# A decoder layer whose matmul order is fixed by hand: ScalarE and VectorE join the fixed order

## The chip, the cores and the metric

The kernel runs on one core of a Trainium2 chip. The metric is the time on the device in microseconds (us) of one execution. Engine names: TensorE (PE in the profile, PEld its weight loads), VectorE (DVE), ScalarE (ACT), GpSimd (POOL), SyncE (SP).

## The reference

One hybrid decoder layer in float32: 256 tokens, width 2048, and a memory of 256 rows.

```python
def reference(x, mem, ...):
    h = x
    h = h + 0.5 * swiglu(rmsnorm(h, g_ffn1), w1_gate, w1_up, w1_down)     # 2048 -> 2 x 5632 -> 2048
    z = rmsnorm(h, g_mix) @ w_in                                          # columns u, v, q, k, v
    y_a = spatial_gating(z[..., :2048], g_v, w_s, b_s)                    # gelu(u) * (causal w_s @ rmsnorm(gelu(v)) + b_s)
    y_b = window_attention_sinks(z[..., 2048:3072], k, v, sinks)          # 16 heads of 64, window 128
    y = concatenate([rmsnorm(y_a, g_a_out), rmsnorm(y_b, g_b_out)])
    h = h + y @ w_out
    h = h + cross_attention(rmsnorm(h, g_x), rmsnorm(mem, g_mem), w_xq, w_xkv, w_xo)   # 4 heads of 512
    h = h + 0.5 * swiglu(rmsnorm(h, g_ffn2), w2_gate, w2_up, w2_down)
    return rmsnorm(h, g_final)
```

## The kernel before

**Precision and tiles.** Each float32 operand is split into a high part (`...h`, a ScalarE cast to fp32r, line 148) and a low part (`...l`, VectorE's difference, line 149); a product takes three passes: high times high, low times high, high times low. The 256 tokens are two blocks of 128. Weights come in chunks of 1 MB (tile 128 x 2048, four pieces of 512 columns), loaded on SP's queue by `load`, which also splits them.

**Units.** A unit is one pass over the chunks of a weight for 1024 output columns by 256 tokens, in four or more PSUM banks named P, Q, R. Three kinds of chunk: N and C have 24 matmuls of 128x512, S has 21 (a seven-product scheme; its `t` tiles are sums of weight pieces). A unit's eight chunks go through `push` and `flush`: `push` of chunk i loads and splits it, then writes the matmuls of chunk i - 1; the last chunk's matmuls come with the `flush()` at the end of `unit`. Only after that do the lines behind `unit(...)` evict the banks (ScalarE with a scale or Gelu, or VectorE's additions), and the next unit's first `push` follows. In the first and last chunk of a unit the matmuls go bank by bank, so the third matmul needs the low part of the weights; in the others the passes with the low part come last.

**Sequence.** f1g (gate and up, 11 units), f1d (down), q, kv, v, u, mv0, mv1, mk0, mk1 (memory values and keys), wo, xq (2 units), xo, f2g, f2d. Between them lie `side` generators (transposes, attention, norms) of which `side_step` runs a piece at every sixth matmul; `yield n` puts the next piece n steps later. In units v, u and mv0 these are the window attention (scores `sc`, softmax in `scs`, transposes `pT`, copies `pTs`, products `wop`) and, in u, the normalised memory pairs `mT` by `pair_normalized`.

**What sets the order.** `tc.manual_schedule(engines={PE})`: TensorE's instructions run in program order. The order on ScalarE, VectorE, GpSimd and the DMA queues is a scheduler's, by dependencies and priorities (`tc.high_priority()` stands around the evictions); it may place an instruction ahead of others written before it. Within each engine's built order the hardware's queue is worked off from the front.

**The first unit.** `plain_gu_unit` works on `n0`, x in transposed form without the norm factor, while `prep1(i)` loads `xT` pairs and x itself into `h`, squares it (`parts1`), makes the norm factor and scales rows (`n1s`) for the units that follow.

Of the kernel before, what the change touches and what calls it, by code (L numbers as in the profile page):

```python
# [14 lines left out]
P = 128  # L15
T = 256
# [5 lines left out]
NEG = -1e30  # L22
NG = D // 512


# [5 lines left out]
def layer_kernel(  # L31
# [22 lines left out]
    nc = tc.nc  # L54
    ctx.enter_context(tc.manual_schedule(engines={mybir.EngineType.PE}))

# [18 lines left out]
    def s2(s):  # L75
        return tmp.tile([P, 512], F32, tag="s2", name=nm(s))
# [163 lines left out]

    def pair_from_dram(s, srcT, i, gcol, base=None, raw=None):
        if raw is None:
            raw = s2(s + "r").rearrange("p (k t) -> p k t", k=2)
            nc.sync.dma_start(raw, srcT[i * T:(i + 1) * T, :].rearrange("(k p) t -> p k t", p=P))
# [7 lines left out]
    def pair_normalized(s, kind, srcT, i, gcol, by_token):  # L252

        raw = s2(s + "r").rearrange("p (k t) -> p k t", k=4)
        src = srcT[i * T:(i + 1) * T, :].rearrange("(k p) t -> p k t", p=P)
        for tb in range(TB):
            a, b = laid(kind, 0, tb), laid(kind, 1, tb)
            nc.gpsimd.dma_start(raw[:, a:b + 1:b - a, :], src[:, :, tb * P:(tb + 1) * P])
        turned = 1 if kind == "S" else 0
        for k in range(2):  # L260
            c = gcol + 2 * i + k
            o = row_tile(kind, raw, k)
            nc.vector.scalar_tensor_tensor(
                out=o, in0=o, scalar=sm[:, c:c + 1], in1=by_token[:, turned:turned + 2, :],
                op0=ALU.mult, op1=ALU.mult,
            )
        p = Pair(s, kind)
        fill(s, p, raw)
        return p
# [28 lines left out]
    def load(s, w, kind, pieces):  # L298
# [5 lines left out]
        if kind == "S":  # L304
# [256 lines left out]
    def ffn(s, get, rs, wgu, wd, on_block, first=None):  # L561
# [36 lines left out]
        def gu_unit(c):  # L598
# [12 lines left out]
            for i in range(8):  # L611
                if c == 10 and i > 1:
                    inner(i - 2)
                push(
                    u, i, wgu[i, c], lambda i=i: get(i),
                    lambda i=i: seven_early(u, got) if i == 6 else late(u) if i == 7 else None,
                )
# [46 lines left out]
    def next_norm(s, gcol, kinds="NNNNNNNN"):  # L664
# [11 lines left out]
        def on_block(j, tb):  # L676
            square_into(parts[:, tb, j:j + 1], h[:, tb, j * 512:(j + 1) * 512], 512)
            done[j] += 1
            if not mixed:
                if done[j] == TB:  # L680
                    make(j, lambda tb, c: h[:, tb, c:c + P])
            elif j < 2:
                if done[0] + done[1] == 2 * TB:
                    st["est"] = rstd_of(parts[:, :, :2], 2, 1024)
                    for i in range(2):
                        scaled(i)
            elif done[j] == TB:
                scaled(j)
# [44 lines left out]

    quad = []

    def prep1(i):
# [4 lines left out]
        n0.append(pair_from_dram(  # L741
            "n0", xT, i, G_FFN1, [t[:, i % 2] for t in quad], raw=raw0 if i == 0 else None
        ))
        if i in (2, 3):
            for j in (2 * i - 4, 2 * i - 3):
                hj = h[:, :, j * 512:(j + 1) * 512]
                nc.sync.dma_start(hj, x[:, j * 512:(j + 1) * 512].rearrange("(b p) d -> p b d", p=P))
                for tb in range(TB):
                    square_into(parts1[:, tb, j:j + 1], hj[:, tb, :], 512)
        if i == 4:  # L750
            rs1.append(rstd_of(parts1, NG, D))
        if i >= 4:
            j = i - 4
            r = m4("n1s").rearrange("p (b c) -> p b c", b=TB)
            for tb in range(TB):
                nc.scalar.activation(
                    r[:, tb], h[:, tb, j * 512:(j + 1) * 512], AF.Copy, scale=rs1[0][:, tb:tb + 1]
                )

            def work():  # L760
                for q in range(2):
                    yield 3 if q == 0 else 1
                    n1[2 * j + q] = pair_from_rows(
                        "n1", KINDS[2 * j + q],
                        lambda tb, k: r[:, tb, (2 * q + k) * P:(2 * q + k + 1) * P],
                        G_FFN1 + 4 * j + 2 * q,
                    )

            side_add(work())

# [4 lines left out]
    )  # L775
    mT = []
    partsm = tiny.tile([P, TB, NG], F32, tag="parts", name=nm("parts"))

    def mem_squares(j):
        for tb in range(TB):  # L780
            mr = s2("mr")
            nc.gpsimd.dma_start(mr, mem[tb * P:(tb + 1) * P, j * 512:(j + 1) * 512])
            square_into(partsm[:, tb, j:j + 1], mr, 512)
# [27 lines left out]

    side_add(queries())
    rsm = rstd_of(partsm, NG, D)
    by_token = const.tile([P, 3, P], F32, name="by_token")

    def spread():

        dg = s2("dg")[:, :T].rearrange("p (b t) -> p b t", b=TB)
        for tb in range(TB):
# [138 lines left out]
    rsv = rstd_of(partsv, 2, DA)  # L958
    for tb in range(TB):
        nc.vector.scalar_tensor_tensor(  # L960
            out=v[tb], in0=v[tb], scalar=rsv[:, tb:tb + 1], in1=gv, op0=ALU.mult, op1=ALU.mult
        )
# [13 lines left out]
    def y_pairs(s, rows_, parts, gcol, k0):  # L976
        rs = rstd_of(parts, 2, DA)
        for tb in range(TB):
            nc.vector.tensor_scalar_mul(rows_[tb], rows_[tb], rs[:, tb:tb + 1])
# [171 lines left out]
    for cb in range(2):  # L1151
        both = rows_scaled("xq", unit("xq", w_xq, cb, n3), rs3_())
        for j in range(2):
            side_add(attend_memory(2 * cb + j, both[j]))

    n4, on4, rs4_ = next_norm("n4", G_FFN2, KINDS)
    for cb in range(2):
# [115 lines left out]
```

## Time and profile before

| what | before |
|---|---|
| time, median of 3 runs | 2107.73 us (2104.63 to 2107.79) |
| profiled execution, its own time | 2105.79 us |
| its span | 2104.0 us |
| its mean granted TensorE clock | 0.996 |

The span is what the profiler saw from the first to the last instruction; 1.8 us lie around it. Rows of the timeline give start and duration in us, then engine, line, operation, output from inputs, shape, and, in brackets, how long the engine was idle before and what ended that. Rows that group instructions give minimum, median and maximum in ns. TensorE's durations overlap, since matmuls are pipelined; the distance of their starts is what counts.

### The profile page before, as it was taken

The numbers are of one execution on the slowest core, as the hardware profiler recorded it, in microseconds if no ns is written. First come the engines' busy times: TensorE is split into PE (matmuls) and PEld (weight loads), VectorE is DVE, ScalarE is ACT, GpSimd is POOL, SyncE is SP. The second block draws the span as 40 slices with busy tenths as digits, with TensorE's granted clock in tenths as the row PEclk, the third lists the DMA queues.
The fourth block names the chain that finished last, engine by engine and source line by source line (L and its number), as shares of the span: only waits on it lengthen the run. The fifth ranks groups of instructions, "written<-read, shape, count | busy, mean of one in ns | idle before, by whom it ended". The sixth has DMA issues, their size and how long they took to land.

```text
span 2104.0 us, 23815 instructions
## 1 busy us (share of the span) xinstructions
PE 2076.0 (99%) x9527; PEld 1715.5 (82%) x9527; DVE 1674.5 (80%) x1609; ACT 1135.4 (54%) x1109; POOL 32.2 (2%) x51
## 2 busy tenths in 40 slices
PE   9999999999999999999999999999999999999998
PEld 7888888888888888788888888778888888888886
DVE  5888888888987745867858657798888888889878
ACT  7655555555544645544545455665555545555444
POOL 0000000000000000100000000000000000000000
PEclk9999999999999999999999999999999999999999
DMA  7555555555555554435555543455555555555553
GB/s 281 195 189 213 200 195 184 209 188 199 202 199 206 201 210 166 167 140 200 180 180 184 197 160 140 163 197 200 181 207 197 204 191 200 200 200 200 200 198 122
DMA packets 60110, 402.15 MB, mean 191 GB/s; under 512 B 6864, under 2 KB 8928, under 8 KB 12768
## 3 DMA queue, kind: packets, MB, share of 16 engines
q1 hardware_dynamic: 57280, 393.50, 51.7%
q0 software_dynamic: 2016, 6.30, 0.9%
q8 instruction: 74, 1.21, 0.2%
q10 hardware_dynamic: 704, 0.84, 0.1%
q14 instruction: 36, 0.29, 0.0%
HBM read 398.52 MB, written 2.10 MB: 190 GB/s over the span
## 4 chain that ended last, share of the span: by engine, by line
PE 94%; DVE 3%; ACT 1%; issue 1%; DMA 1%; POOL 0%; SPq 0%; POOLq 0%; DVEq 0%; ACTq 0%
PE f2gQ L363 16%; PE f1gQ L363 15%; PE f1dQ L363 6%; PE f2dQ L363 6%; PE f2gP L363 6%; PE f1gP L363 5%; PE f1dP L363 3%; PE f2dP L363 3%; PE woQ L363 2%; PE xqQ L363 2%; PE f1dR L363 2%; PE f2dR L363 2%; PE xoQ L363 2%; PE mk0Q L363 1%; PE mv1Q L363 1%; PE mv0Q L363 1%
## 5 line engine op out<-in xcount | busy, mean ns | idle before, releaser
L149 DVE TENSOR_TENSOR f1gwl<-f1gw,f1gwh 128x2048 fp32r<-128x2048 f32 (+1 forms) x91 | 185.5, 2043 | 51.6 <-ACT f1gwh L148 51.4
L148 ACT CAST f2gwh<-f2gw 128x1536 fp32r<-128x1536 f32 (+1 forms) x88 | 154.4, 1755 | 133.4 <-PE f2gQ L363 96.6
L148 ACT CAST f1gwh<-f1gw 128x2048 fp32r<-128x2048 f32 (+1 forms) x91 | 156.1, 1716 | 123.5 <-PE f1gQ L363 90.4
L149 DVE TENSOR_TENSOR f2gwl<-f2gw,f2gwh 128x1536 fp32r<-128x1536 f32 (+1 forms) x88 | 183.7, 2088 | 40.3 <-ACT f2gwh L148 40.2
L363 PE MATMUL f2gQ<-f2gwh,n4fh 128*128 128x512 f32 x363 | 141.4, 390 | 0.0
L363 PE MATMUL f2gQ<-f2gwh,n4fl 128*128 128x512 f32 x363 | 141.3, 389 | 0.0
L363 PE MATMUL f1gQ<-f1gwh,n1fh 128*128 128x512 f32 x330 | 128.6, 390 | 0.0
L363 PE MATMUL f1gQ<-f1gwh,n1fl 128*128 128x512 f32 x330 | 128.4, 389 | 0.0
L148 ACT CAST f2dwh<-f2dw 128x2048 fp32r<-128x2048 f32 (+1 forms) x44 | 79.2, 1799 | 91.2 <-PE f2dQ L363 71.2
L148 ACT CAST f1dwh<-f1dw 128x2048 fp32r<-128x2048 f32 (+1 forms) x44 | 79.2, 1799 | 87.9 <-PE f1dQ L363 68.2
L149 DVE TENSOR_TENSOR f2dwl<-f2dw,f2dwh 128x2048 fp32r<-128x2048 f32 (+1 forms) x44 | 94.4, 2145 | 27.0 <-ACT f2dwh L148 24.3
L363 PE MATMUL f2gQ<-f2gwl,n4fh 128*128 128x512 f32 x363 | 115.7, 392 | 0.0
L149 DVE TENSOR_TENSOR f1dwl<-f1dw,f1dwh 128x2048 fp32r<-128x2048 f32 (+1 forms) x44 | 94.3, 2144 | 26.8 <-ACT f1dwh L148 24.2
L363 PE MATMUL f1gQ<-f1gwl,n1fh 128*128 128x512 f32 x330 | 105.1, 392 | 0.0
L149 DVE TENSOR_TENSOR f2gtl<-f2gt,f2gth 128x2048 fp32r<-128x2048 f32 x33 | 75.6, 2292 | 17.0 <-ACT f2gth L148 16.6
L149 DVE TENSOR_TENSOR f1gtl<-f1gt,f1gth 128x2048 fp32r<-128x2048 f32 x30 | 68.8, 2292 | 18.3 <-ACT f1gth L148 18.0
L363 PEld LDWEIGHTS f2gQ<-f2gwh,n4fl 128*128 128x128 f32 x363 | 68.1, 188 | 14.2
L363 PEld LDWEIGHTS f2gQ<-f2gwh,n4fh 128*128 128x128 f32 x363 | 68.2, 188 | 14.1
L363 PEld LDWEIGHTS f2gQ<-f2gwl,n4fh 128*128 128x128 f32 x363 | 67.3, 188 | 13.5
L148 ACT CAST f2gth<-f2gt 128x2048 fp32r<-128x2048 f32 x33 | 63.1, 1913 | 23.1 <-DVE f2gt L314 18.3
L363 PEld LDWEIGHTS f1gQ<-f1gwh,n1fl 128*128 128x128 f32 x330 | 62.0, 188 | 12.9
L363 PEld LDWEIGHTS f1gQ<-f1gwh,n1fh 128*128 128x128 f32 x330 | 62.0, 188 | 12.8
(703 smaller groups left out, 5715.1 us busy)
## 6 DMA issues: line engine op xcount, KB each, us to landing
f2gw<-in_w_gu SPq DMA_DIRECT2D x88, 1024.0 KB, 4.8
f1gw<-in_w_gu SPq DMA_DIRECT2D x87, 1024.0 KB, 4.8
f1dw<-in_w_down SPq DMA_DIRECT2D x44, 1024.0 KB, 4.8
f2dw<-in_w_down SPq DMA_DIRECT2D x44, 1024.0 KB, 4.8
wow<-in_w_out SPq DMA_DIRECT2D x16, 1024.0 KB, 4.8
xqw<-in_w_xq SPq DMA_DIRECT2D x16, 1024.0 KB, 4.8
xow<-in_w_xo SPq DMA_DIRECT2D x16, 1024.0 KB, 4.8
qw<-in_w_in SPq DMA_DIRECT2D x8, 1024.0 KB, 5.0
```

The source lines that it names most:

```text
L148: nc.scalar.copy(hi, src)
L149: nc.vector.tensor_tensor(lo, src, hi.bitcast(F32), ALU.subtract)
L363: nc.tensor.matmul(self.banks[name], x, y, start=name not in self.begun, stop=self.left[name] == 0)
```

## The change

ScalarE and VectorE are added to the engines that follow program order. Since the program's order then decides when they do something, some of the program is moved:

- `prep1`: x goes into `h` in four DMAs from GpSimd at i = 1 to 4 (before: two by two from SyncE at i = 2, 3); the next `xT` pair is loaded one step ahead; the norm factor is made at i = 5, the scaling of rows (`normalized`) at i = 6 and 7, two blocks each.
- `load`, kind S: the three additions for `t` stand ahead of the split of the other pieces.
- `ffn`: the norm factor is taken at chunk 5 of the first unit; `next_norm` scales the first two blocks in a side generator, two steps later.
- q unit: `beside_queries` loads rows of `mem` a step ahead of their squares and takes the norm factor at i = 3; the last squares come behind the unit. `spread` and `y_pairs` begin with a `yield 2`.
- u unit: `beside_u` scales v at i = 1; the `memT` blocks are loaded a chunk ahead of the pair that uses them, so that the last two pairs fall into mv0.
- xq: the norm factor is taken at i = 3. `shared.clear()` is called twice more.

```diff
+PINNED = {mybir.EngineType.PE, mybir.EngineType.DVE, mybir.EngineType.Activation}
-    ctx.enter_context(tc.manual_schedule(engines={mybir.EngineType.PE}))
+    ctx.enter_context(tc.manual_schedule(engines=PINNED))
...
     def load(s, w, kind, pieces):
...
-            split(wh[:, 1:, :], wl[:, 1:, :], raw[:, 1:, :])
             nc.vector.tensor_tensor(
                 t[:, 0:2, :], raw[:, 1:3, :], raw[:, 0:1, :].to_broadcast([P, 2, 512]), ALU.add
             )
             nc.vector.tensor_tensor(t[:, 2, :], t[:, 0, :], raw[:, 2, :], ALU.add)
             nc.vector.tensor_tensor(t[:, 3, :], t[:, 2, :], raw[:, 3, :], ALU.add)
+            split(wh[:, 1:, :], wl[:, 1:, :], raw[:, 1:, :])
             split(th, tl, t)
...
     def prep1(i):
...
+        raw = ahead.pop()
+        if i < 7:
+            ahead.append(s2("n0r").rearrange("p (k t) -> p k t", k=2))
+            nc.sync.dma_start(ahead[0], rows_of(xT, i + 1))
+        n0.append(pair_loaded("n0", raw, i, G_FFN1, [t[:, i % 2] for t in quad]))
+        if 1 <= i <= 4:
+            cols = slice((i - 1) * 512, i * 512)
+            nc.gpsimd.dma_start(h[:, :, cols], x[:, cols].rearrange("(b p) d -> p b d", p=P))
+        if 2 <= i <= 5:
+            for tb in range(TB):
+                square_into(parts1[:, tb, i - 2:i - 1], h[:, tb, (i - 2) * 512:(i - 1) * 512], 512)
+        if i == 5:
+            rs1.append(rstd_of(parts1, NG, D))
+        for j in {6: (0, 1), 7: (2, 3)}.get(i, ()):
+            normalized(j)
...
-    pq = unit("q", w_in, 2, n2, lambda i: mem_squares(i // 2) if i % 2 else None)
+    pq = unit("q", w_in, 2, n2, beside_queries)
...
+    def beside_u(i):
+        if i == 1:
+            for tb in range(TB):
+                nc.vector.scalar_tensor_tensor(
+                    out=v[tb], in0=v[tb], scalar=rsv[:, tb:tb + 1], in1=gv, op0=ALU.mult, op1=ALU.mult
+                )
+        beside_mT(i)
+
+    def beside_mT(i):
+        if loaded:
+            mT[i - 2] = pair_normalized("mT", KINDS[i - 2], loaded.pop(), i - 2, G_MEM, by_token)
+        if 1 <= i <= 8:
+            loaded.append(load_blocks("mT", KINDS[i - 1], memT, i - 1))
...
-    pu = unit("u", w_in, 0, n2, lambda i: mT.append(pair_normalized("mT", KINDS[i], memT, i, G_MEM, by_token)))
+    pu = unit("u", w_in, 0, n2, beside_u)
...
-    pv_ = unit("mv0", w_xkv, 2, mT)
+    pv_ = unit("mv0", w_xkv, 2, mT, lambda i: beside_mT(8 + i) if i < 2 else None)
```

Where work lands on the engines is read from the built instruction orders. ScalarE where unit v ends and u begins, before (`v` the Gelu evictions, `junk` the squares, `uwh` u's weights; line numbers are those of each kernel's own file):

```order
L148 CAST vwh_6006<-vw_6005 128x2048
L148 CAST uwh_6124<-uw_6123 128x2048
L900 ACTIVATE scs_6026,den_5861<-scs_6026,nmx_6032 128x128 x4
L956 ACT_TABLE_LOAD
L956 ACTIVATE v_5731<-vP_997_5746,rs_5557 128x512
L956 ACTIVATE v_5731<-vQ_998_5747,rs_5557 128x512
L138 ACTIVATE junk_6088,partsv<-v_5731 128x512
L138 ACTIVATE junk_6091,partsv<-v_5731 128x512
L956 ACTIVATE v_5732<-vR_5748,rs_5557 128x512
L148 CAST uwh_6145<-uw_6144 128x2048
L138 ACTIVATE junk_6094,partsv<-v_5732 128x512
L956 ACTIVATE v_5732<-vQ_1000_5749,rs_5557 128x512
```

And in the changed kernel at the same place:

```order
L985 ACTIVATE v_5731<-vP_997_5746,rs_5359 128x512
L140 ACTIVATE junk_6088,partsv<-v_5731 128x512
L985 ACTIVATE v_5731<-vQ_998_5747,rs_5359 128x512
L140 ACTIVATE junk_6091,partsv<-v_5731 128x512
L985 ACTIVATE v_5732<-vR_5748,rs_5359 128x512
L140 ACTIVATE junk_6094,partsv<-v_5732 128x512
L985 ACTIVATE v_5732<-vQ_1000_5749,rs_5359 128x512
L140 ACTIVATE junk_6097,partsv<-v_5732 128x512
L150 CAST uwh_6109<-uw_6108 128x2048
L150 CAST uwh_6120<-uw_6119 128x2048
```

Both of u's first casts stood ahead of v's last eviction; now both stand behind it and behind the last square.

ScalarE where u ends and mv0 begins, before (`u` the evictions, `scs` exponentials of the window attention, `mT` pairs of the normalised memory):

```order
L900 ACTIVATE scs_6451,den_6257<-scs_6451,nmx_6457 128x256 x2
L148 CAST mTfh_6472<-mTr_6467 128x512
L148 CAST mv0wh_6638<-mv0w_6637 128x2048
L148 CAST mTfh_6474<-mTf_6476 128x512
L969 ACT_TABLE_LOAD
L969 ACTIVATE u_6107<-uP_1073_6150,rs_5557 128x512
L969 ACTIVATE u_6107<-uQ_1074_6151,rs_5557 128x512
```

And in the changed kernel:

```order
L929 ACTIVATE scs_6592,den_6230<-scs_6592,nmx_6598 128x256 x2
L1009 ACT_TABLE_LOAD
L1009 ACTIVATE u_6105<-uP_1064_6125,rs_5359 128x512
L1009 ACTIVATE u_6105<-uQ_1065_6126,rs_5359 128x512
L1009 ACTIVATE u_6106<-uR_6127,rs_5359 128x512
L1009 ACTIVATE u_6106<-uQ_1067_6128,rs_5359 128x512
L150 CAST mTfh_6612<-mTr_6504 128x512
L150 CAST mTfh_6614<-mTf_6616 128x512
L150 CAST mv0wh_6628<-mv0w_6627 128x2048
```

The first cast for mv0 stood ahead of u's evictions; now it stands behind all four, behind two casts of an `mT` pair, and these behind the exponentials of the last scores (`scs_6592`), whose scores TensorE computes after u's last matmul.

VectorE where mv1 ends and mk0 begins, before (`mv` the sums that evict mv1, `mk0wl` the low part of mk0's first weights):

```order
L149 TENSOR_TENSOR mk0wl_7298<-mk0w_7296,mk0wh_7297 128x2048
L484 TENSOR_TENSOR mv1v_7258<-mv1Q_1251_7105,mv1p_1270_7257 128x512
L490 TENSOR_TENSOR mv_6635<-mv1P_1236_7031,mv1p_1270_7257 128x512
L485 TENSOR_TENSOR mv1z_7259<-mv1Q_1250_7104,mv1v_7258 128x512
L310 TENSOR_TENSOR mk0t_7340<-mk0w_7336 128x1024
```

And in the changed kernel:

```order
L497 TENSOR_TENSOR mv1v_7260<-mv1Q_1239_7034,mv1v_7260 128x512
L498 TENSOR_TENSOR mv_6609<-mv1Q_1240_7035,mv1v_7260 128x512
L499 TENSOR_TENSOR mv_6608<-mv1Q_1241_7036,mv1z_7261 128x512
L151 TENSOR_TENSOR mk0wl_7300<-mk0w_7298,mk0wh_7299 128x2048
L151 TENSOR_TENSOR mk0wl_7306<-mk0w_7304,mk0wh_7305 128x2048
```

The low part of mk0's weights moved from ahead of mv1's sums to behind the last of them.

More of the change, by code (lines that the diff above doesn't have):

```diff
@@ L613, in gu_unit @@
                     inner(i - 2)
+                if c == 0 and i == 5:
+                    rs()
                 push(
@@ L684, in on_block, with first @@
                     st["est"] = rstd_of(parts[:, :, :2], 2, 1024)
-                    for i in range(2):
-                        scaled(i)
+                    def first():
+                        yield 2
+                        for i in range(2):
+                            scaled(i)
+                    side_add(first())
             elif done[j] == TB:
@@ L734, in layer_kernel @@
     quad = []
+    ahead = [raw0]
     def prep1(i):
@@ L740, in prep1 @@
             ]
[L741 to L750, printed above, removed]
-            rs1.append(rstd_of(parts1, NG, D))
@@ L752, in prep1 @@
[L752 to L757, printed above, removed]
-                )
[L760 to L769, printed above, removed]
+        raw = ahead.pop()
@@ new lines, in prep1, with normalized, work @@
+        if i == 5:
+            rs1.append(rstd_of(parts1, NG, D))
+        for j in {6: (0, 1), 7: (2, 3)}.get(i, ()):
+            normalized(j)
+    def normalized(j):
+        r = m4("n1s").rearrange("p (b c) -> p b c", b=TB)
+        for tb in range(TB):
+            nc.scalar.activation(
+                r[:, tb], h[:, tb, j * 512:(j + 1) * 512], AF.Copy, scale=rs1[0][:, tb:tb + 1]
+            )
+        def work():
+            for q in range(2):
+                yield 3 if q == 0 else 1
+                n1[2 * j + q] = pair_from_rows(
+                    "n1", KINDS[2 * j + q],
+                    lambda tb, k: r[:, tb, (2 * q + k) * P:(2 * q + k + 1) * P],
+                    G_FFN1 + 4 * j + 2 * q,
+                )
+        side_add(work())
@@ L775, in layer_kernel, with beside_queries @@
     )
-    mT = []
+    mT = [None] * 8
+    shared.clear()
     partsm = tiny.tile([P, TB, NG], F32, tag="parts", name=nm("parts"))
[L779 to L783, printed above, removed]
+    loaded = []
+    def beside_queries(i):
+        if i == 3:
+            rs2_()
+        if loaded:
+            for tb, mr in enumerate(loaded):
+                square_into(partsm[:, tb, i // 2 - 1:i // 2], mr, 512)
+            loaded.clear()
+        if i % 2 and i < 8:
+            j = i // 2
+            for tb in range(TB):
+                loaded.append(s2("mr"))
+                nc.gpsimd.dma_start(loaded[tb], mem[tb * P:(tb + 1) * P, j * 512:(j + 1) * 512])
     qs = [m4("qs") for _ in range(TB)]
     qT = [None] * 2
-    pq = unit("q", w_in, 2, n2, lambda i: mem_squares(i // 2) if i % 2 else None)
+    pq = unit("q", w_in, 2, n2, beside_queries)
     rs2 = rs2_()
@@ L977, in y_pairs @@
         rs = rstd_of(parts, 2, DA)
+        yield 2
         for tb in range(TB):
@@ L1151, in layer_kernel @@
     for cb in range(2):
-        both = rows_scaled("xq", unit("xq", w_xq, cb, n3), rs3_())
+        both = rows_scaled("xq", unit("xq", w_xq, cb, n3, lambda i: rs3_() if i == 3 else None), rs3_())
         for j in range(2):
             side_add(attend_memory(2 * cb + j, both[j]))
+    shared.clear()
     n4, on4, rs4_ = next_norm("n4", G_FFN2, KINDS)
```

22 lines of the change are left out of this document (12 added, 10 removed).

## The prediction

> **What bounds the kernel now.** I read the page first, then TensorE's waits, then the places in the timeline where one unit of work ends and the next begins, then the windows around the two stretches in which TensorE lost time. The page's busy times and its chain:
>
> ```profile
> PE 2076.0 (99%) x9527; PEld 1715.5 (82%) x9527; DVE 1674.5 (80%) x1609; ACT 1135.4 (54%) x1109; POOL 32.2 (2%) x51
> PE 94%; DVE 3%; ACT 1%; issue 1%; DMA 1%; POOL 0%; SPq 0%; POOLq 0%; DVEq 0%; ACTq 0%
> ```
>
> TensorE is the bound. A change that alters no matmul can gain only what TensorE waits, and loses whatever it makes TensorE wait. All it waits for now (first, second and last of 14 rows; the 14 add up to 17.5 us):
>
> ```profile
> PE wop L918 <- DVE pTs L913: 4.8, 2, 4.6
> PE f1gP L363 <- DVE n0l L143: 1.9, 1, 1.9
> PE n L218 <- DVE n2fl L143: 0.5, 1, 0.5
> ```
>
> None is at the end of a unit. The next rows show why: the timeline where unit `v` ends and `u` begins (start, duration, both in us).
>
> ```profile
> 827.06 1.91 ACT L148 CAST uwh<-uw 128x2048 fp32r<-128x2048 f32 x1 [4.74 <-issue]
> 829.01 2.29 DVE L149 TENSOR_TENSOR uwl<-uw,uwh 128x2048 fp32r<-128x2048 f32 x1 [2.56 <-ACT uwh L148]
> 830.54 1.28 ACT L956 ACT_TABLE_LOAD   x1
> 831.84 0.69 ACT L956 ACTIVATE v<-vP,rs 128x512 f32<-128x512 f32 x1
> 834.22 0.68 ACT L956 ACTIVATE v<-vR,rs 128x512 f32<-128x512 f32 x1
> 834.33 0.39 PE L363 MATMUL vQ<-vwl,n2fh 128*128 128x512 f32 x1
> 834.56 0.39 PE L363 MATMUL uP<-uwh,n2fh 128*128 128x512 f32 x1
> 834.79 0.39 PE L363 MATMUL uP<-uwh,n2fl 128*128 128x512 f32 x1
> 835.01 0.39 PE L363 MATMUL uP<-uwl,n2fh 128*128 128x512 f32 x1
> 836.59 0.64 ACT L138 ACTIVATE junk<-v 128x512 f32<-128x512 f32 x1
> 837.12 0.20 ACT L138 ACTIVATION_READ_ACCUMULATOR junk<-v 128x1 f32 x1
> ```
>
> `u`'s first weights were split (827.06 to 831.30) before any eviction of `v`; TensorE goes from `vQ` to `uP` at its steady 0.227 us. The third matmul of a first chunk already needs the low half `uwl`.
>
> **The change, at the ends of units.** TensorE's program is nearly unchanged, so is every count of work on ScalarE and VectorE. What changes is who waits behind whom. `unit()` ends with `flush()`, its evictions follow in the program, and only then comes the first `push` of the next unit. In the order now built, the first cast of the next unit stands behind the last eviction of the old one, which needs TensorE's last matmul (the order rows of `v` to `u` above). Call E the moment at which TensorE could go on. The last result is out 0.16 us later (0.39 less 0.227), and a follower starts about 0.05 after. The durations:
>
> ```profile
> L792 ACT ACTIVATE qs<-qQ,rs x2: 675/682/690, 765.6 to 770.0; 128x512 f32<-128x512 f32 x2
> L1022 ACT COPY mv<-mv0Q x2: 580/584/589, 954.4 to 958.7; 128x512 f32<-128x512 f32 x2
> L1041 ACT ACTIVATE xq<-xqQ,rs x4: 687/690/690, 1220.9 to 1283.3; 128x512 f32<-128x512 f32 x4
> L514 DVE SCALAR_TENSOR_TENSOR h<-f1dQ,h x16: 681/684/692, 528.5 to 722.9; 128x512 f32<-128x512 f32 x16
> L693 ACT ACTIVATE n4s<-h,rs x8: 709/712/717, 1349.3 to 1392.8; 128x512 f32<-128x512 f32 x8
> L837 DVE TENSOR_SCALAR kd<-kv,rs x4: 341/341/350, 782.0 to 783.0; 128x128 f32<-128x128 f32 x4
> L491 DVE TENSOR_TENSOR mv<-mv1Q,mv1z x1: 684/684/684, 997.3 to 997.3; 128x512 f32<-128x512 f32 x1
> ```
>
> Rows of one engine follow each other some 0.09 sooner than their durations say (829.01 + 2.29 against the next row).
>
> - Plain eviction on ScalarE: E + 0.2, eviction 0.6, cast 1.9, `wl` 2.29 and a handoff: the third matmul runs at E + 5.0 instead of E + 0.45. TensorE loses 4.6 us, 4.5 with COPY: mv0 to mv1, mk1 to wo, xq to xq, xq to xo, together 18.2.
> - With more between: add on VectorE and square (0.64 + 0.20) for f1d to q and wo to xq, 5.5 each; Gelu and square for v to u, 5.4; add, square and two `n4s` for xo to f2, 6.8. Together 23.2.
> - q to kv: two squares of `mem` (about 0.72 each: 0.64 + 0.20 less the overlap) stand between: 6.2. The second kv chunk's cast stands behind the last `qT` copy, twelve short matmuls ahead of its use: 0.6 + 1.9 + 2.3 less 1.5 is 3.3. Together 9.5.
> - Only VectorE held (mv1 to mk0, mk0 to mk1; the cast is free): E + 0.2, add 0.6, `wl` 2.29, less 0.45: 2.7 each. kv to v: three scalings of 0.34: 3.0. Together 8.4.
> - u to mv0 is the worst. In the order above the exponentials of the last scores stand ahead of u's evictions, and those scores are computed after u's last matmul.
>
> What a softmax step and a pair of `mT` take, from one chunk of `u`:
>
> ```profile
> 861.73 0.68 DVE L889 SCALAR_TENSOR_TENSOR scs<-sc,band 128x512 f32<-128x512 f32 x1
> 862.45 0.69 DVE L893 TENSOR_REDUCE mx<-scs 128x2 f32<-128x512 f32 x1
> 863.44 0.16 DVE L898 TENSOR_SCALAR nmx<-mx 128x2 f32<-128x2 f32 x1
> 864.18 0.50 ACT L900 ACTIVATE scs<-scs,nmx 128x256 f32<-128x256 f32 x1
> 865.08 0.19 ACT L900 ACTIVATION_READ_ACCUMULATOR scs<-scs,nmx 128x1 f32 x1
> 867.42 0.62 ACT L148 CAST mTfh<-mTr 128x512 fp32r<-128x512 f32 x1 [2.16 <-DVE mTr L263]
> 867.95 0.40 ACT L148 CAST mTfh<-mTf 128x256 fp32r<-128x256 f32 x1
> 868.34 1.90 ACT L148 CAST uwh<-uw 128x2048 fp32r<-128x2048 f32 x1
> L363 PE MATMUL uP<-uwh,n2fh x16: 389/389/497, 834.6 to 894.8; 128*128 128x512 f32 x16
> ```
>
> Softmax on VectorE 1.9, exponentials 1.1, table 1.3, four evictions 2.4, two casts of `mT` 1.1, cast 1.9, `wl` 2.3, from the end of the scores: 12.1 with a handoff, less the 0.45: 11.6 us.
>
> Inside `u` the same things form a ring: `uwl` 2.2, softmax 1.9, exponentials 1.1, `mT` casts 1 to 2, next cast 1.9, in all 8 to 9 us. The last row gives the room: first to last chunk 60.2, less the 8.0 lost there today and 0.7 within the last chunk, is 7.4 a chunk on average, 5.9 (24 x 0.227 and one set of transposes) in the short ones. Followed chunk by chunk, two come late, by 0.6 and 3.2. I take 4, with 0 to 14 as ends. In `f1g` and `f2g`, followed through the new order with these durations, each cast keeps over 1 us of room, in `f1d` and `f2d` nearly so; I cost them at nothing; the memory attention's extra matmuls give its casts time too. The rest moves work that has room: `rs` at i = 5 or 3, `spread` and `y_pairs` a step later, the three additions ahead of the split, four `h` loads from SP's queue to GpSimd's, the `memT` loads a chunk earlier on GpSimd's. A chunk of TensorE covers each; uncovered, each costs its own duration once, which the ends below allow.
>
> Sum of the ends and of `u`: 18.2 + 23.2 + 9.5 + 8.4 + 11.6 + 4 = 75.
>
> **The first unit.** The activations `h` (2 MB) now come by GpSimd's queue beside the first weights, on a full DMA (0.98 and 1.04 in the first windows below); four scalings `n1s` and `n0h` stand ahead of chunk 7's cast.
>
> ```profile
> L756 ACT ACTIVATE n1s<-h,rs x8: 707/714/722, 29.4 to 49.6; 128x512 f32<-128x512 f32 x8
> 38.00:42.00 4.00, 1.56 (x4) 1.05 (x5) 4.00 (x6) 1.74 (x5) 0.00 (x0) 0.86 0.98 335
> 40.00:44.00 4.00, 3.05 (x10) 2.47 (x10) 2.23 (x5) 0.00 (x0) 0.00 (x0) 0.61 1.04 375
> 845.00:850.00 5.00, 0.47 (x3) 0.04 (x1) 4.97 (x8) 1.54 (x5) 1.44 (x2) 0.98 0.35 103
> 850.00:857.00 7.00, 6.96 (x20) 5.39 (x21) 5.00 (x13) 2.54 (x7) 1.44 (x2) 0.52 0.42 151
> ```
>
> (Columns: length, busy PE, PEld, DVE, ACT, POOL with counts, granted clock, DMA share, GB/s.) Early `n0h` takes away the loss at 38 to 42: 2.4 of waiting and, at half clock for about 3.4, 1.7 more. Against it: 512 KB of `h` ahead of chunk 1 is 1.5 at 335 GB/s; the weights' piece waits 1.0 behind `n0h`; 4 x 0.7 + 2 x 0.45 ahead of casts at two places, by my reckoning 2.6 and 3.9 late. Net +4.9; the ends are -4 (all hidden) and +9 (none gained). I take +4.
>
> **What it removes.** The wait at 845 to 850 (4.6) and the half clock after it (0.52 over 7 us, 3.4 lost), 8.0; of the other waits, by the earlier loads, scalings and norm factors, 4 of 10. In all -12, between -4 and -17.
>
> **The clock.** Both stretches of waiting above were followed by half clock: 2.4 us of waiting cost 1.7 more, 4.6 us cost 3.4. At a dozen places TensorE will now wait 2.7 to 11.6 us. I take the smaller price at each, +20; ends 0 and 41.
>
> **Sum.** 75 + 4 - 12 + 20 = +87 on the profiled execution's 2105.8 (span 2104.0), 1.9 under the median of the runs: 2193.
>
> **Rivals.** First, the clock holds: one early wait is split into 2.7 and 2.2 us by two matmuls, so TensorE shows work in each stretch. Against it, in 38 to 42 the clock fell although TensorE was busy 1.56 of 4.00. It would give 2105.8 + 67 = 2173. [...]
>
> Second, the ring in `u` and the same ring in mv0 (gate, squares, exponentials) turn slower than TensorE in every chunk: 2 to 3 us in 12 chunks more, and the larger clock price: 2193 + 30 + 15 = about 2238.
>
> Third, the other side: the late casts hide. That decides if the next unit's start is worth under 1.3 us: 12 + 4 gained, over 13 ends. It would need the cast or TensorE to have other work there. Where transposes stand in a unit's first chunk they come after its 12th matmul, so they cover nothing. If the whole were covered: 2105.8 - 16 = about 2090. That the order is not followed at all I exclude: the built order of before agrees row by row with its trace at `v` to `u`.
>
> **How the numbers follow.** The sum with its clock price 0.62 (2193, own range 2178 to 2218), the clock holding 0.20 (2173), the slow rings 0.11 (2238), the covered ends 0.05 (2090), an even trade 0.02. A fifth at most is left out from 2155, where the ends also cost 10 less and the rings nothing, to 2232, the middle of the ring's case. Within 0.2% (4 us) is about what a measurement of this kernel cannot tell from no change: faster 0.05, same 0.02, slower 0.93.
>
> **What would show it.** After the change, TensorE's waits should list `qwh`, `kvwh`, `uwh`, `mv0wh`, `mv1wh`, `wowh`, `xqwh`, `xowh`, `f2gwh` on ScalarE and the same names' `wl` on VectorE, 2.5 and 2.2 us each; the cast should start after the last eviction; the granted clock should dip behind these; the gate-and-up units stay without waits. The prediction is wrong if the casts still start ahead of the old unit's end, or if TensorE does not wait there.

## The result, and the profile after

| what | before | after |
|---|---|---|
| time, median | 2106.71 us (4 runs, 2104.63 to 2107.79) | 2287.07 us (4 runs, 2285.71 to 2288.37) |
| profiled span | 2104.0 us | 2284.8 us |
| mean granted TensorE clock | 0.996 | 0.967 |
| TensorE's listed waits | 17.5 us in 14 rows | 138.3 us in 44 rows |

The ratio is 1.0857, with a 95% interval of 1.0839 to 1.0876. The forecast was 2193 us (2155 to 2232): the sign was right, and the loss is 180 us where 87 were forecast. Of the span's 180.8 us, 138.3 less 17.5, that is 120.8, are listed waits of TensorE. For another 51 it worked at half clock: the trace's clock records have 26 stretches at half clock (0.50 granted) in after, 143.4 us together (before: 2 stretches, 10.2 us), in which TensorE was busy for 111.7 us (before: 10.0), and half of that time is lost, 55.9 against 5.0. Of the 9 that are left, some 5 are, as an estimate, the first matmul behind a wait: its follower starts 0.33 us after it (at 900.07 below) and not 0.227, and there are 50 waits more than before. Another 1.7 lie behind TensorE's last matmul. One of the six executions of e10 below took 2300.07 us and is left out of its interval.

The busy times on the page after:

```profile
PE 2134.5 (93%) x9527; PEld 1747.5 (76%) x9527; DVE 1694.9 (74%) x1609; ACT 1129.9 (49%) x1109; POOL 34.1 (1%) x55
```

TensorE has the same 9527 matmuls; it is busy 58 us longer for them and waits 6% of the span. What it waits for, some of the 44 rows (total, times, longest, in us):

```profile
PE mv0P L368 <- ACT mv0wh L150: 11.1, 1, 11.1
PE f2gP L368 <- ACT f2gwh L150: 9.0, 2, 5.0
PE uP L368 <- ACT uwh L150: 6.3, 2, 3.3
PE xqP L368 <- ACT xqwh L150: 5.9, 2, 3.3
PE f1gP L368 <- ACT f1gwh L150: 5.7, 2, 4.5
PE f1gP L368 <- DVE f1gwl L151: 4.9, 4, 1.9
...
PE f1dP L368 <- DVE f1dwl L151: 4.1, 4, 1.3
...
PE f1dP L368 <- ACT f1dwh L150: 3.7, 2, 2.0
...
PE f1dP L368 <- DVE f1gp L495: 3.0, 1, 3.0
...
PE vP L368 <- ACT vwh L150: 0.2, 1, 0.2
```

The high and low parts of weights stand behind 108 of the 138 us, most of them with the name of a unit's first bank (`P`). The rows of `v` to `u`, the place that the prediction showed of before:

```profile
896.36 0.39 PE L368 MATMUL vQ<-vwl,n2fh 128*128 128x512 f32 x1
896.79 0.69 ACT L985 ACTIVATE v<-vQ,rs 128x512 f32<-128x512 f32 x1
897.51 0.63 ACT L140 ACTIVATE junk<-v 128x512 f32<-128x512 f32 x1
...
898.13 3.69 ACT L150 CAST uwh<-uw 128x2048 fp32r<-128x2048 f32 x2
...
900.05 2.29 DVE L151 TENSOR_TENSOR uwl<-uw,uwh 128x2048 fp32r<-128x2048 f32 x1 [1.43 <-ACT uwh L150]
900.07 0.50 PE L368 MATMUL uP<-uwh,n2fh 128*128 128x512 f32 x1 [3.32 <-ACT uwh L150]
...
902.39 0.80 PE L368 MATMUL uP<-uwl,n2fh 128*128 128x512 f32 x1 [1.59 <-DVE uwl L151]
...
902.99 0.63 PE L368 MATMUL uP<-uwh,n2fh 128*128 128x512 f32 x1
```

The cast that ended at 828.97 before, 5.4 us ahead of `vQ`'s last matmul, now starts at 898.13, 1.8 us after it. TensorE waits 3.32 us for the high part and 1.59 for the low one. The last row starts 0.60 us after the one before it, where 0.227 was the pace; the ones behind it follow at 0.43: half clock, since 900.93 by the clock records. The windows behind this end and at mv0's start (busy PE, PEld, DVE, ACT, POOL, granted clock, DMA share, GB/s):

```profile
896.00:903.00 7.00, 2.09 (x8) 1.09 (x7) 3.28 (x4) 6.92 (x9) 0.71 (x1) 0.85 0.02 6
903.00:910.00 7.00, 7.00 (x27) 5.57 (x26) 5.69 (x8) 0.85 (x3) 1.47 (x2) 0.66 0.80 255
979.00:986.00 7.00, 5.86 (x14) 4.18 (x15) 5.65 (x7) 2.73 (x3) 0.00 (x0) 0.50 0.44 151
```

From 903 to 910 TensorE has work the whole time and gets through 27 matmuls; the clock is 0.66.

Three kinds of wait the prediction had priced at nothing. The first is in the down projection, whose chunks also take the gate's result apart (`f1af`):

```profile
641.05 2.29 DVE L151 TENSOR_TENSOR f1dtl<-f1dt,f1dth 128x2048 fp32r<-128x2048 f32 x1 [0.31 <-ACT f1dth L150]
643.26 0.42 DVE L202 TENSOR_TENSOR f1af<-f1a 128x256 f32<-128x256 f32 x1
...
644.51 0.29 DVE L208 TENSOR_TENSOR f1af<-f1a,f1af 128x128 f32<-128x128 f32 x1
644.84 0.62 ACT L150 CAST f1afh<-f1af 128x512 fp32r<-128x512 f32 x1 [3.31 <-DVE f1af L208]
645.37 1.89 ACT L150 CAST f1dwh<-f1dw 128x2048 fp32r<-128x2048 f32 x1
...
647.31 0.50 PE L368 MATMUL f1dP<-f1dwh,f1afh 128*128 128x512 f32 x1 [1.73 <-ACT f1dwh L150]
```

ScalarE idles 3.31 us for VectorE's small sums, which stand behind `f1dtl`, and the cast of the next weights stands behind ScalarE's: a ring over two engines, and TensorE waits 1.73 us. The second is a chunk of kind S, whose three additions now stand ahead of the low part. In such a chunk, too, and not only in a unit's first and last, the third matmul needs the low part:

```profile
487.22 1.22 DVE L314 TENSOR_TENSOR f1gt<-f1gw 128x1024 f32<-128x1024 f32 x1
...
489.81 1.75 DVE L151 TENSOR_TENSOR f1gwl<-f1gw,f1gwh 128x1536 fp32r<-128x1536 f32 x1
...
491.61 0.50 PE L368 MATMUL f1gP<-f1gwl,n1fh 128*128 128x512 f32 x1 [1.93 <-DVE f1gwl L151]
```

From 487.22 to 489.81 VectorE adds, and TensorE, two matmuls into the chunk, waits 1.93 us for what follows. There are seven waits of this kind, 7.3 us. The third is a bank that is emptied late:

```profile
502.31 2.29 DVE L151 TENSOR_TENSOR f1dwl<-f1dw,f1dwh 128x2048 fp32r<-128x2048 f32 x1 [1.12 <-ACT f1dwh L150]
504.52 0.68 DVE L495 TENSOR_TENSOR f1gp<-f1gP,f1gp 128x512 f32<-128x512 f32 x1
505.36 0.77 PE L368 MATMUL f1dP<-f1dwh,f1afh 128*128 128x512 f32 x1 [2.99 <-DVE f1gp L495]
```

The sum that empties `f1gP` stands behind the next low part, so `f1dP`, in the same bank, waits 2.99 us.

### The profile page after: what moved, and what is told of

Same layout as the page of the kernel before. It is cut to its first block, busy times and chain, and to the rows that moved or that the text cites. A ratio compares the mean times of both kernels' runs of the same rounds, so it can differ in the third digit from the quotient of the medians.

```text
span 2284.8 us, 23830 instructions
## 1 busy us (share of the span) xinstructions
PE 2134.5 (93%) x9527; PEld 1747.5 (76%) x9527; DVE 1694.9 (74%) x1609; ACT 1129.9 (49%) x1109; POOL 34.1 (1%) x55
## 5 line engine op out<-in xcount | busy, mean ns | idle before, releaser
L151 DVE TENSOR_TENSOR f2dwl<-f2dw,f2dwh 128x2048 fp32r<-128x2048 f32 (+1 forms) x44 | 94.2, 2143 | 27.8 <-ACT f2dwh L150 26.6
L150 ACT CAST f1gth<-f1gt 128x2048 fp32r<-128x2048 f32 x30 | 57.4, 1914 | 83.2 <-DVE f1gt L318 83.2
L151 DVE TENSOR_TENSOR f2gtl<-f2gt,f2gth 128x2048 fp32r<-128x2048 f32 x33 | 75.7, 2293 | 11.7 <-ACT f2gth L150 11.6
L368 PE MATMUL f2gP<-f2gwh,n4fh 128*128 128x512 f32 x176 | 70.3, 400 | 9.0 <-ACT f2gwh L150 9.0
```

The lines of the kernel that those rows point to most:

```text
L150: nc.scalar.copy(hi, src)
L151: nc.vector.tensor_tensor(lo, src, hi.bitcast(F32), ALU.subtract)
L368: nc.tensor.matmul(self.banks[name], x, y, start=name not in self.begun, stop=self.left[name] == 0)
```

## The experiments

A run is compared with runs of the kernel before on its chip, whose medians lie from 2104.7 to 2106.1 us. Where no interval is given there was one run, and a difference of under 2 us between two of them says nothing. The table puts the measurements together. Half clock is from the clock records, without the stretch at the end, behind TensorE's last matmul; the loss is half of the time that TensorE was busy in these stretches.

| run | time, us | span | TensorE's waits | mean clock | half clock: stretches, us | loss, us |
|---|---|---|---|---|---|---|
| after | 2287.07 | 2284.8 | 138.3 | 0.967 | 26, 143.4 | 55.9 |
| e1 moves only | 2095.25 | 2093.6 | 13.5 | 0.998 | 1, 3.4 | 1.6 |
| e10 and x on SyncE | 2092.57 | 2091.4 | 10.6 | 0.998 | 1, 3.4 | 1.7 |
| e3 TensorE, ScalarE fixed | 2236.68 | 2235.0 | 104.3 | 0.972 | 19, 119 | 44.9 |
| e4 TensorE, VectorE fixed | 2217.81 | 2216.1 | 97.4 | 0.982 | 14, 68 | 25.6 |
| e5 weights ahead | 2201.94 | 2200.2 | 82.6 | 0.983 | 14, 68.3 | 29.6 |
| e8 fills behind | 2272.84 | 2271.1 | 131.9 | 0.970 | 23, 126.3 | 49.4 |
| e9 both | 2188.51 | 2186.8 | 78.5 | 0.987 | 11, 47.8 | 21.0 |
| e6 busy waits | 2308.35 | 2306.6 | 74.1 | 0.983 | 17, 68.3 | 31.4 |
| e11 half as busy | 2261.29 | 2259.6 | 86.5 | 0.987 | 10, 51.2 | 23.1 |
| e12 x on SyncE | 2279.78 | 2278.1 | 132.9 | 0.968 | 27, 139.9 | 55.4 |
| e13 split first | 2406.88 | 2405.2 | 201.9 | 0.961 | 33, 180.9 | 71.6 |
| e14 all edits | 2315.24 | 2313.2 | 144.6 | 0.976 | 19, 105.8 | 41.6 |
| e15 all but the split | 2191.78 | 2190.1 | 76.0 | 0.984 | 13, 61.4 | 26.6 |
| e16 u's last chunk | 2203.61 | 2201.9 | 78.5 | 0.981 | 20, 75.1 | 36.5 |

**e1: the moves, without the fixed order.**

```diff
-PINNED = {mybir.EngineType.PE, mybir.EngineType.DVE, mybir.EngineType.Activation}
+PINNED = {mybir.EngineType.PE}
```

> The changed program with only TensorE held to program order, so with all its moved loads, norm factors and side work, but ScalarE and VectorE ordered by the scheduler. Theory A (the fixed order on ScalarE and VectorE makes the loss, by putting the next weights' casts behind evictions and fills): the 120 us of added waits and the half clock go, and the time is within 10 us of before, about 2110, some microseconds lost at the start where the four loads of x by GpSimd's queue run beside the first weights. Rival B (the moved loads and norm factors carry a good part of the loss): above 2140.

Measured: 2095.25 us (2094.83 to 2096.26) against 2105.71, ratio 0.9953 (0.9936 to 0.9969). The moved loads and factors alone gain 10 us, and the whole loss is the order of ScalarE and VectorE. One long wait is new, at the start, since x now comes on GpSimd's queue beside the first weights:

```profile
PE f1gP L368 <- ACT f1gwh L150: 4.5, 1, 4.5
```

**e3 and e4: which of the two engines.**

```diff
-PINNED = {mybir.EngineType.PE, mybir.EngineType.DVE, mybir.EngineType.Activation}
+PINNED = {mybir.EngineType.PE, mybir.EngineType.Activation}    # e3
+PINNED = {mybir.EngineType.PE, mybir.EngineType.DVE}           # e4
```

> The changed program with TensorE and ScalarE held to program order and VectorE free. Theory A: the waits behind ScalarE's casts at unit ends stay (about 55 us, and their low halves with them), those behind VectorE's sums and low halves in the down projections and at mk0 and mk1 go (about 40 us), as does a third of the half clock: about 2215. Rival: the rings through both engines need both fixed, and one free engine dissolves nearly all: under 2150.

> The changed program with TensorE and VectorE held to program order and ScalarE free. Theory A: casts go ahead of evictions again, the low halves stay behind VectorE's sums: at f1d to q, mv1 to mk0, mk0 to mk1, wo to xq, xo to f2 and kv to v about 2.7 us each, and some in the down projections, 25 us of waits and 15 us of clock: about 2150. Rival as for the run with ScalarE fixed: either engine alone costs nearly nothing, under 2125.

Measured: 2236.68 (2215 was expected) and 2217.81 (2150 was expected). Fixing ScalarE alone costs 141 us on e1, VectorE alone 123, both 192: they do not add up, and VectorE costs far more than the 8.4 us of its own ends in the forecast. In e4 the waits have VectorE's names, at the same places:

```profile
PE mv0P L368 <- DVE mv0wl L151: 8.6, 1, 8.6
PE uP L368 <- DVE uwl L151: 8.5, 2, 7.5
```

The low part also stands behind the old unit's work, and while one engine's half is late it does not help that the other's is early.

**e5: the next unit's first weights ahead of the last matmuls of the old one**, at 13 ends.

```diff
+    def preload(nxt):
+        ready.append(load(*nxt, None) ...)
...
-            b = load(u.s, w, u.kinds[i], pieces)
+            b = ready.pop() if i == 0 and ready else load(u.s, w, u.kinds[i], pieces)
...
     def unit(s, w, cb, pairs, beside=None, nxt=None):
...
+        preload(nxt)
         flush()
```

> The changed kernel, all three engines fixed, with one edit: the first weights of the next unit are loaded and split ahead of the old unit's last matmuls and evictions in the program (13 unit ends, the two kv chunks among them). Theory A (the head of the queue at unit ends): of the 72 us of waits there some 60 go, u to mv0 keeps about 6 since TensorE then waits for u's banks; the half clock at these places goes too, another 25 to 30: about 2195. Rival: the wait moves from the cast to the PSUM banks, which are still evicted late, and only 20 to 30 us are gained: about 2260.

Measured: 2201.94, 85 us less. This is the direct test of the ends: with the load written ahead of `flush()`, 55.7 us of waits go and 75 us of half clock, which are 26 us of loss. Of mv0's 11.1 us half stays, now for the eviction of u that frees the bank, and the start and the inside of f1d are as they were:

```profile
PE mv0P L368 <- ACT u L1025: 5.5, 1, 5.5
PE f1gP L368 <- ACT f1gwh L150: 5.7, 2, 4.6
PE f1dP L368 <- DVE f1dwl L151: 4.1, 4, 1.3
```

**e8 and e9: the ring of the down projections.** The pieces that take the gate's result apart (`inner`) are written behind `push`, in the down projections as shown and in the last gate-and-up unit likewise; in e8 alone, in e9 together with e5.

```diff
-                for ahead in seq[at:at + 7]:
-                    inner(ahead)
-                at += 1
                 push(u, q, wd[i, half], ...)
+                for ahead in seq[at:at + 7]:
+                    inner(ahead)
+                at += 1
```

> The changed kernel, all three engines fixed, with one edit: in the down projections and the last gate-and-up unit the fills of activation pairs (inner) stand behind the load and split of the next weights in the program, not ahead of them. Theory D (the part of the loss that the forecast left out is a ring: the cast of a fill waits for VectorE's sums, these stand behind the low half of the last weights, and the next weights' cast stands behind the fill): the waits on f1dwh, f2dwh, f1dwl, f2dwl and at the last gate-and-up unit fall by 15 to 20 us and the half clock behind them by about 10: about 2258. Rival (VectorE simply has too much to do there, in whatever order): within 8 us of 2287.

> The two edits together: first weights of the next unit ahead of the old unit's last matmuls, and fills behind the weights. If the two causes are apart, the gains add: 85 us of the first edit and what the second gives alone, about 2172. Rival: both dissolve the same waits, and the sum is less than the larger alone plus half the smaller, above 2185.

Measured: 2272.84, 14 us less than after, and 2188.51, 13 less than e5: the place of `inner` is worth 13 to 14 us, with e5's edit and without it. Not all of it is the ring. In e8 the waits fall by 6.4 us and the loss at half clock by 6.5. The two waits for the banks (`f1gp`, `f2gp`) are gone, 5.8 us; of those for S chunks' low parts 2.7 of 7.3 us stay; those for the casts `f1dwh` and `f2dwh` are 5.2 us where they were 7.4, at other chunks than before. Against that, new waits have come in the last chunks of the gate-and-up units, for `f1gwh` and `f2gwh` (1.9 us each) and the low parts behind them (1.3 and 1.6). What the ring alone costs was not separated.

**e6 and e11: the price of the clock.** Idle matmuls on a spare bank stand in front of the first and third matmul of twelve units (in `v` and `mk0` of the third alone), so that TensorE works where it would wait. The results are not used.

```diff
+                if first and n in (0, 2):
+                    fill_in(self.s, n)
...
+            for _ in range(k):      # e6: 28 and 13 for u, 96 and 9 for mv0; e11: half of each
+                nc.tensor.matmul(fps[:, :P], ones, ones, start=True, stop=True)
```

> The changed kernel with idle matmuls (128 columns, about 0.11 us each, into a spare bank that nobody reads) put into TensorE's order where it waits at 11 starts of units: as many before the first matmul and after the second as fit into the waits measured there (28 and 13 at u, 96 and 9 at mv0, and so on). They end before what TensorE waits for comes, so no wait grows. Theory C (a wait costs its length and then a stretch of half clock on top): the half clock behind these 11 places goes and the time falls by about 28 us, to 2259; the waits at other places keep theirs. Rival (the granted clock falls for another reason, such as what the chip draws): no change, 2287, or more by what the idle matmuls take.

Measured: 2308.35, 21 us more. The row shows why: 28 matmuls in front of `uP` are 56 in the trace and take 6.41 us, where the wait was 3.32.

```profile
896.95 6.41 PE L406 MATMUL fill<-ones 128*128 128x128 f32 x56
```

A float32 matmul of 128 columns is two instructions here, 0.23 us together; I had counted one. e6 overfilled the waits, so that its time settles nothing about the price; the half clock fell even so, to 68.3 us. e11 has half as many:

> The run with idle matmuls again, with half as many at each place (14 and 6 at u, 48 and 4 at mv0, and so on), since each float32 one took 0.23 us in two passes, not 0.11, and so ran past the waits. Theory C: TensorE is kept busy in the waits and none grows; the half clock behind the 11 places goes and the time falls by about 28 us against the changed kernel, to 2259. Rival (half clock there costs nothing that the waits do not cost already): within 5 us of 2287.

Measured: 2261.29, 26 us less than after, with nothing taken away that TensorE waited for. Unit `u` starts 6.35 us earlier here, at 893.72, so the same two windows as above begin at 889.65 (ScalarE and VectorE do in the first what they did there, 6.92 and 3.28 us):

```profile
889.65:896.65 7.00, 6.54 (x49) 5.87 (x48) 3.28 (x4) 6.92 (x9) 0.71 (x1) 1.00 0.01 5
896.65:903.65 7.00, 7.00 (x37) 5.67 (x36) 6.79 (x10) 1.05 (x4) 1.47 (x2) 1.00 0.82 283
```

The clock stays at 1.00, and the second window holds 37 matmuls instead of 27. The half-clock time falls from 143.4 to 51.2 us, the loss from 55.9 to 23.1; waits and idle matmuls together are some 7 us longer than the waits were, which takes part of it back. So at these twelve starts of units the clock alone cost at least 26 us, more than the 20 that I had put down for all.

**e10 and e12: x on SyncE's queue**, in e10 with only TensorE fixed, in e12 with all three.

```diff
-            nc.gpsimd.dma_start(h[:, :, cols], ...)
+            nc.sync.dma_start(h[:, :, cols], ...)
```

> Only TensorE fixed, with the moved loads and norm factors, and one edit: the four loads of x go by SP's queue in their place among the weights, not by GpSimd's. Theory E (by GpSimd's queue all four are issued in the first 6 us and hold up the first weights, 4.5 us of waiting in the run with only TensorE fixed): that wait falls to under 1.5 us and the time to about 2091. Rival (the wait is bandwidth alone, and x has to come early anyway): within 2 us of 2095.

> The changed kernel, all three engines fixed, with the four loads of x by SP's queue in their place among the weights. Theory E: the wait of 4.5 us for the second chunk's weights falls to about 1.5 and the half clock of 6.8 us behind it goes: 5 to 7 us less, about 2281. Rival: within 2 us of 2287.

Measured: e10 2092.57, ratio 0.9933 (0.992 to 0.9946) against before in five rounds, the best version here; e12 2279.78, 7 less than after. In after, the four loads leave GpSimd one behind the other, the first at 2.68 and the rest from 3.95 to 6.12 (first row), and the second chunk's cast waits for its weights until 17.36:

```profile
3.95 2.17 POOL L761 DMA_DIRECT2D h<-in_x  x3
...
17.36 1.90 ACT L150 CAST f1gwh<-f1gw 128x2048 fp32r<-128x2048 f32 x1 [5.79 <-DMA f1gw<-in_w_gu]
```

In e10 the wait of e1 is down from 4.5 to 1.6 us at most:

```profile
PE f1gP L368 <- ACT f1gwh L150: 2.0, 2, 1.6
```

**e13: the split ahead of the additions**, as the kernel before has it, in the otherwise changed kernel.

```diff
+            split(wh[:, 1:, :], wl[:, 1:, :], raw[:, 1:, :])
             nc.vector.tensor_tensor(
                 t[:, 0:2, :], raw[:, 1:3, :], ...
...
-            split(wh[:, 1:, :], wl[:, 1:, :], raw[:, 1:, :])
             split(th, tl, t)
```

> The changed kernel with one of its own moves undone: in chunks of kind S the split of the weights stands ahead of the three additions again. Theory F (with VectorE fixed, 2.6 us of additions ahead of the low half make the third matmul of S chunks wait 1.3 to 1.9 us at some 14 places: f1gwl, f1dwl, f2dwl, f2gwl, xowl, wowl, mk0wl): these waits of about 18 us go, with a little half clock, and some come back at the low half of the sums (f1gtl, f1dtl), which are needed 8 to 17 matmuls later: about 2272. Rival (the move was right for a fixed order: without it the sums' low half is later still): 2287 or more.

Measured: 2406.88, 120 us more, where I had expected a gain.

```profile
PE f1gP L368 <- DVE f1gwl L151: 8.5, 12, 1.6
PE f2gQ L368 <- ACT f2gth L150: 8.0, 12, 2.7
...
PE f1gQ L368 <- ACT f1gth L150: 7.0, 10, 2.7
```

In this order the additions come behind the subtraction, so the cast `f1gth` is late on ScalarE and everything behind it there too. Nearly every gate-and-up unit now waits for it, and for the next `wl` besides. Of the 120 us, 63.6 are listed waits and 15.7 the clock; the rest was not split up. Under a fixed order this move was needed: it exchanges a few waits of 1 to 2 us for these.

**e14, e15, e16: the rest together.** e14 has all the edits with e13's; e15 has e9, x on SyncE, the units' side work written behind `push` (in the first unit too), and no side steps in u's last chunk; e16 is e5 with the last of these alone.

```diff
-        u = Unit(s, "N" * 8)
+        u = Unit(s, "N" * 8, alone=(7,) if s == "u" else ())    # e14, e15, e16
         for i in range(8):
-            if beside is not None:
-                beside(i)
             push(u, i, w[i, cb], lambda i=i: have(pairs, i))
+            if beside is not None:                                # e14, e15
+                beside(i)
```

> All three engines fixed, and all edits so far together: first weights of the next unit ahead, fills and work beside a unit's chunks behind the weights, the split ahead of the additions, x by SP's queue, and no side work in u's last chunk (so no scores ahead of u's evictions). Theory A to F: the waits of 78 us left with the first two edits fall by 18 (split), 5 (x) and 15 (u, mv0, first unit), the clock's cost by 12: about 2140, above before since some rings stay. Rival (a fixed order on three engines cannot come near, since two engines wait for one another in every chunk with sums): above 2170.

> The run with all edits, but with the additions ahead of the split as in the changed kernel. Theory G (the rest are rings that go when side work stands behind the weights): x by SP's queue gives 7, no scores in u's last chunk 5, and the work beside the chunks of u, mv0, q, xq and the first unit behind their weights 10: from 2188.5 to about 2165. Rival H (in a fixed order one engine's late item only changes its place: what stood ahead of the weights and is now behind them is late itself): 2180 or more, with new waits on n0h, n1r, n4r and mT.

> The run with the next unit's first weights ahead (2201.9), and in addition no side work in u's last chunk, so that the last scores are computed after mv0's first matmuls and their exponentials stand behind u's evictions. Theory A: the wait of 5.5 us of mv0 for u's eviction falls under 2 and its half clock goes: about 2196. Rival (u's evictions are late by themselves, behind the table load and the casts of the last pair): within 2 us of 2202.

Measured: 2315.24, 2191.78 and 2203.61. e14 differs from e15 by the split alone, and is 123 us slower: e13's loss once more. e15 is no better than e9 (2188.51): waits have gone and others have come.

```profile
PE f1gP L368 <- ACT n0h L144: 5.2, 2, 2.9
PE f1a L220 <- ACT f1a L595: 4.4, 1, 4.4
```

In e16 mv0 waits 1.3 us for u's eviction instead of 5.5; inside mv0, at the window attention's last transposes, 2.6 us are waited where e5 has 2.1. The total of waits falls by 4.1, but the half clock rises from 68.3 to 75.1 us and its loss by 6.9, and the time does not move. One case of that: a wait of 2.7 us for `uwh` inside u is in both, and half clock sets in during it in e16 (at 920.52, the wait ends at 921.27) and not in e5 (it ends at 919.86). The two waits first named, in e16:

```profile
PE pT L954 <- DVE scs L934: 2.6, 1, 2.6
PE mv0P L368 <- ACT u L1025: 1.3, 1, 1.3
```

So in e15, with weights first, late side work takes the place of late weights, and in e16 the clock takes back what the wait gave. What the 76 to 79 us of waits that remain in e9 and e15 would need was not found.

## Why the prediction was half right

**The ends and u: right.** Forecast 75, measured 72.6 in the waits of after.

| place | forecast | measured |
|---|---|---|
| f1d to q, wo to xq | 5.5 each | 4.9 each |
| q to kv, with the second kv chunk | 9.5 | 8.2 |
| kv to v | 3.0 | 3.1 |
| v to u | 5.4 | 4.9 |
| inside u | 4 | 2.9 |
| u to mv0 | 11.6 | 12.2 |
| mv0 to mv1, mk1 to wo | 4.5, 4.5 | 3.6, 4.1 |
| mv1 to mk0 | 2.7 | 2.5 |
| mk0 to mk1 | 2.7 | 6.8 |
| xq to xq, xq to xo | 4.6 each | 4.2 each |
| xo to f2 | 6.8 | 6.1 |

(The sum uses unrounded rows.) Only mk0 to mk1 is far off: 3.5 is the low part, where 2.7 were forecast, and 3.3 a bank that `mk`'s sums on VectorE had not emptied. That the casts would stand behind the last eviction is what the rows at 896 show and what e5 confirms.

**"I cost them at nothing": wrong, and the larger part of the miss.** The step followed the casts on ScalarE through f1g, f2g, f1d and f2d and let a chunk of TensorE cover the rest. For the gate-and-up units in the middle this held: from 92 to 489 us and from 1569 to 2011 TensorE waits nowhere. Waits outside the ends and u are 65.7 us in after; the forecast left some 10. They are the first unit to 92 us (about 15), the end of f1g with f1d (15.5), xo with the first unit of f2g (15), the end of f2g with f2d (12.6), mk0 and wo (6.4). Three things were missing. A cast was taken as late by its own queue alone, while ScalarE's next instruction there waits for VectorE's sums (the ring at 641 to 647). The three additions of an S chunk were judged as work that a chunk covers, but an S chunk itself needs the low part for its third matmul. And a bank was taken to be free at its unit's end, while the sum that empties it stands behind the next low part. e4 shows the same from the other side: VectorE's order alone costs 123 us.

**The clock: half clock behind the waits right, the size not.** "I take the smaller price at each, +20" stands against 51, by the loss at half clock of after less that of before. Two factors miss: 26 stretches where 12 were counted, since half clock sets in at uncounted waits too (at 504.98 and 662.00 in f1d) and some ends wait twice, and a larger price for each (55.9 us over 26 stretches, 2.15 each) where 1.7 was taken. e11 shows at least 26 us of it in the time itself. The rival that the clock holds is refuted: 2173 stands against 2287, and the clock fell at 900.93, behind u's 3.32 us wait, although two matmuls split it from the next.

**What it removes, -12: right.** e1 measures 10.5 us of gain, with the wait at 845 to 850 gone; in it the first unit's waits are up by 2.9 us, so some 13 us were gained at other places. **The first unit, +4: too small.** Its waits up to 92 us grew from 4.7 to 15.7 us. The one of 4.5 us for the second chunk, behind x, was named at 1.5, for the 512 KB of one load; all four, 2 MB, had left GpSimd by 6.12. e12 shows 7 us for the queue alone.

**The other rivals.** The slow rings were put into u and mv0, where little of it came (2.9 us in u); rings of the same form turned in f1d and f2d. The covered ends are refuted by every row of the waits.

The price of each part, then: 87 forecast, about +56 for waits costed at nothing, about +31 for the clock, 9 in neither, less 2 at the ends: 181.

## What to carry to other kernels

When an engine is put into program order, write out for each of its instructions what it stands behind now, on every such engine, and follow a chain across two engines rather than each queue alone; what a scheduler had found by itself must then be written out as the order of the program. Where weights are prepared for a bound engine, the preparation belongs ahead of the last results of the work before it (85 of 180 us here), and the moves that make the order tenable are worth trying without the order: they gave 0.5%, and 0.7% with x on another queue. A stretch of half clock behind waits on TensorE cost about 2 us more here (55.9 us over 26 stretches), and whether a wait was followed by one is not told by its length alone, as the next section shows (1.94 us was, 2.53 was not); so compare waits and half clock together.

## What the runs showed of the hardware

The 26 half-clock stretches of after last 3.41 us (15 of them), 6.83 (8), 10.24 (2) and 17.07 (1). Waits of up to about 1.9 us mostly did not bring one (1.93 us at 489 did not, 1.94 at 2011 did), waits of 2.4 to 3.3 mostly did (2.53 at 1087 did not). Windows of 3.41 us around the waits just named:

```profile
487.92:491.33 3.41, 1.76 (x8) 1.13 (x6) 3.34 (x4) 1.38 (x2) 0.00 (x0) 1.00 0.18 74
1085.26:1088.67 3.41, 1.96 (x9) 1.30 (x7) 2.67 (x4) 1.90 (x1) 0.00 (x0) 1.00 0.00 0
1088.67:1092.08 3.41, 2.34 (x10) 1.96 (x11) 3.41 (x3) 0.00 (x0) 0.00 (x0) 1.00 0.38 89
2010.26:2013.67 3.41, 1.47 (x7) 0.93 (x6) 3.00 (x4) 2.10 (x2) 0.00 (x0) 1.00 0.00 0
2013.67:2017.09 3.42, 3.42 (x10) 2.64 (x9) 3.42 (x3) 3.12 (x4) 0.00 (x0) 0.50 0.82 290
```

Around the wait of 1.93 us TensorE works for 1.76 of 3.41 us, and no half clock follows. The wait of 2.53 us lies across two windows, with 1.96 and 2.34 us of work, and none follows either. Around the one of 1.94 TensorE works for 1.47 us, and the next window has a clock of 0.50; at `v` to `u` it works for 0.73 us from 897.52 to 900.93, where half clock begins. In the 3.41 us ahead of each of the 26 stretches of after it worked for 0.00 to 1.47 us, but for 2.1 ahead of one. This is read from matmul rows, whose ends are modelled. No run varied the length or the place of one wait alone, so what decides whether half clock follows a wait was not shown.
